# Activation and weight tiles placed at other addresses in the four feed-forward blocks of a decoder trunk

## The chip, the cores and the metric

The kernel runs on one core of a Trainium2 chip. The metric is the device time of one execution in microseconds. The on-chip buffer that the engines read has 128 partitions; an address below is a byte offset within a partition, and it is the same on all 128.

## What is computed

The reference is a decoder trunk of two layers over 256 tokens of width 1024, in float32. Each layer is a feed-forward block, a token mixer with memory attention beside it, and a second feed-forward block. Cut to what matters here:

```python
D_MODEL, SEQ, DEPTH = 1024, 256, 2
D_FF = 256 * ((8 * D_MODEL // 3 + 255) // 256)      # 2816

def swiglu(x, w_in, w_out):
    gate, up = jnp.split(x @ w_in, 2, axis=-1)
    return (jax.nn.silu(gate) * up) @ w_out
...
    for i in range(DEPTH):
        x = x + 0.5 * swiglu(rms_norm(x, ffn1_norm_g[i]), ffn1_w_in[i], ffn1_w_out[i])
        hn = rms_norm(x, mix_norm_g[i])
        ...  # projection, mixer (mLSTM or windowed attention), memory heads, output projection
        x = x + 0.5 * swiglu(rms_norm(x, ffn2_norm_g[i]), ffn2_w_in[i], ffn2_w_out[i])
```

## The kernel before, in words

**Layout.** Activations are kept transposed: 128 features on the partitions, 256 tokens along a row, eight such chunks for the width of 1024. A matmul loads a 128x128 piece of a weight matrix as its stationary operand and streams a 128x256 activation chunk past it; the sum grows in a bank of the accumulation memory. In some groups of the mixers (`rows=True`) the roles are exchanged: a 128x128 piece of the activation is loaded and 256 columns of the weight stream.

**Three products for one.** To keep float32 precision with the faster fp32r matmul, each operand is split into a high part, rounded to fp32r, and a low part, the rest. `mm3` (L224 to L228) issues high by high (L225), high weight by low activation (L226) and low weight by high activation (L227). The activation's parts are made in `Norm.put` (L269 to L280) by `split_gain` (L239), for the input half of a block; the hidden units' parts are made in `hidden` (in `ffn_in`) by `split_plain` (L244) into tiles `u`, for the output half.

**Weights.** `wtile` (L216 to L219) starts a DMA of 128x1024 floats on SyncE's queue into a raw tile `wr` (5 buffers), then `split` (L206 to L214) has ScalarE write the high part into a `wh` tile (L211) and VectorE the low part into a `wl` tile (L212); each of these has 8 buffers, in pools of their own. One weight tile feeds 24 matmuls.

**A feed-forward block** (`ffn`, L509) has two halves. The input half (`ffn_in`, L471) goes through 11 groups of 256 hidden units; each needs four weight tiles (two halves of the width, gate and up). The output half goes through four column blocks of 256 with six weight tiles each (22 hidden chunks); after each, the residual is added and the next block's `Norm.put` is called. `Norm.chain` (L293) runs a little later, among the next block's first matmuls: two matmuls against ones (L296) for the sum of squares, a power on GpSimd, and, after a pause, the broadcast of the inverse root over all partitions by fp32 matmuls (`bcast_rows`, helper `mmf`, L231). An fp32 matmul appears as four passes in the trace.

**Order.** TensorE and SyncE run in the order in which the program issues. A helper class (`Weave`) interleaves side chains, such as `Norm.chain`, by a running clock that each matmul advances. The order is fixed when the program is built. The blocks run as: memory keys and values, block 1, mixer A, block 2, block 3, mixer B, block 4.

**Where tiles lie.** A pool's tiles lie one behind the other, and the pools in the order in which they are made, behind the constants. Before, that order is constants, `xhp` and `xlp` (four tiles of 2,048 bytes each), `up` (31 tiles of 2,048), `vp` (two of 2,080), `wrp` (five of 4,096), `whp` and `wlp` (eight of 4,096 each), `tp`, `sp` (4,864 bytes in all), and small ones. The constants end at byte 28,608.

Of the kernel before, what the change touches and what calls it, by code (L numbers as in the profile page):

```python
# [11 lines left out]
F32R = mybir.dt.float32r  # L12
# [7 lines left out]
P = 128  # L20
T = 256
D = 1024
FF = 2816
# [25 lines left out]
G_MEM, G_F1, G_MIX, G_F2, G_XQ, G_XK, G_AH, G_BQ, G_BK, G_END = 0, 8, 24, 40, 56, 58, 60, 68, 69, 70  # L49
# [6 lines left out]


WARM = 18


class Weave:
# [37 lines left out]
def tile_trunk(ctx: ExitStack, tc: tile.TileContext, a, out):  # L99
# [3 lines left out]
    def mk(pool, shape, dt, tag):  # L103
        seq[0] += 1
        return pool.tile(shape, dt, tag=tag, name=f"{tag}_{seq[0]}")

    def pool(name, bufs, **kw):
        return ctx.enter_context(tc.tile_pool(name=name, bufs=bufs, **kw))

    cst = pool("cst", 1)  # L110
    wv = Weave()


    xhp = pool("xhp", 4)
    xlp = pool("xlp", 4)
    up = pool("up", 31)
    vp = pool("vp", 2)
    wrp = pool("wrp", 5)
    whp = pool("whp", 8)
    wlp = pool("wlp", 8)  # L120
    tp = pool("tp", 7)
    sp = pool("sp", 2)
    ap1 = pool("ap1", 1)
    gp = pool("gp", 1)
    cp = pool("cp", 24)
# [73 lines left out]
    def g(i):  # L199
        return gcol[:, i:i + 1]  # L200
# [2 lines left out]
    pieces = [1]  # L203
    last = [None]

    def split(src, shape):  # L206
        hi = mk(whp, shape, F32R, "wh")
        lo = mk(wlp, shape, F32R, "wl")
        n = shape[1] // pieces[0]
        for i in range(pieces[0]):  # L210
            last[0] = nc.scalar.copy(hi[:, i * n:(i + 1) * n], src[:, i * n:(i + 1) * n])  # L211
            tt(out=lo[:, i * n:(i + 1) * n], in0=src[:, i * n:(i + 1) * n],  # L212
               in1=hi[:, i * n:(i + 1) * n].bitcast(F32), op=ALU.subtract)
        return hi, lo  # L214

    def wtile(src, nk, ncol=256):  # L216
        raw = mk(wrp, [P, nk, ncol], F32, "wr")
        nc.sync.dma_start(raw, src)
        return split(raw, [P, nk, ncol])  # L219

    def wcols(w, c0, kh):
        return wtile(w.rearrange("(k p) f -> p k f", p=P)[:, kh * 4:(kh + 1) * 4, c0:c0 + 256], 4)

    def mm3(ps, wh, wl, xh, xl, start, stop):  # L224
        nc.tensor.matmul(ps, wh, xh, start=start, stop=False, skip_group_check=True)  # L225
        nc.tensor.matmul(ps, wh, xl, start=False, stop=False, skip_group_check=True)  # L226
        nc.tensor.matmul(ps, wl, xh, start=False, stop=stop, skip_group_check=True)  # L227
        wv.now += 0.328  # L228
# [10 lines left out]
    def split_gain(src, gc, hi, lo):  # L239
        act(hi, src, AF.Copy, scale=gc)  # L240
        nc.vector.scalar_tensor_tensor(out=lo, in0=src, scalar=gc, in1=hi.bitcast(F32),
                                       op0=ALU.mult, op1=ALU.subtract)
# [18 lines left out]
    class Norm:  # L261


        def __init__(self, gi, rows=True, half=True):
            self.gi, self.rows, self.half, self.rc = gi, rows, half, None
            self.done = False
            self.xT, self.xh, self.xl = [], [], []

        def put(self, xn):  # L269
            c2 = len(self.xT)  # L270
            hi, lo = mk(xhp, [P, 2, T], F32R, "xh"), mk(xlp, [P, 2, T], F32R, "xl")
            for m in range(2):
                split_gain(xn[:, m], g(self.gi + 2 * c2 + m), hi[:, m], lo[:, m])
            self.xh.append(hi)
            self.xl.append(lo)
            self.xT.append(xn)
            self.square(xn, c2 == 0)
            if c2 == 3:
                self.fold()
# [115 lines left out]

    kT = [mk(cst, [P, 2, T], F32, f"kT{i}") for i in range(2)]
    vM = mk(cst, [P, 2, 512], F32, "vM")
    x0 = Norm(G_F1)

    def memory():  # L400

# [2 lines left out]
        bank = mo()  # L404
        for i in range(WARM):
            nc.tensor.matmul(bank, idle[:, :P], idle, start=True, stop=True, skip_group_check=True)
# [61 lines left out]

    KG = [(0, 4), (4, 4), (8, 4), (12, 4), (16, 4), (20, 2)]

    def ffn_in(x, w_in, hh, hl, mid=None):  # L471

        def hidden(ps):
            t = tmp()
            for m in range(2):
                tt(out=t[:, m], in0=ps[m][:, :T], in1=x.rb, op=ALU.mult)  # L476
            act(t, t, AF.Silu)
            for m in range(2):
                tt(out=t[:, m], in0=t[:, m], in1=ps[m][:, T:], op=ALU.mult)  # L479
            hi, lo = unit(F32R), unit(F32R)  # L480
            split_plain(t, hi, lo)
            hh.append(hi)
            hl.append(lo)

        waiting = []
        for gi in range(11):
            ps = [mo(), mo()]
            for kh in range(2):
                for part in range(2):
                    wh, wl = wcols(w_in, part * FF + gi * 256, kh)  # L490
                    for m in range(2):
                        for k in range(4):
                            kc = kh * 4 + k
                            mm3(ps[m][:, part * T:(part + 1) * T],
                                wh[:, k, m * P:(m + 1) * P], wl[:, k, m * P:(m + 1) * P],
                                x.xh[kc // 2][:, kc % 2], x.xl[kc // 2][:, kc % 2],
                                start=kc == 0 and part == 0, stop=kc == 7)
                        yield
            waiting.append(ps)
            if gi == 0 and not x.done:  # L500
                continue
            yield x.ready
            for ps in waiting:
                hidden(ps)
            waiting.clear()
            if mid is not None and gi == 5:
                wv.spawn(mid())

    def ffn(x, w_in, w_out, nxt=None, mid=None):  # L509

        pieces[0] = 1
        hh, hl = [], []
        yield from ffn_in(x, w_in, hh, hl, mid)
        w = w_out.rearrange("(k p) f -> p k f", p=P)

        def products(ps, m, kg, wt, start):
            ms = slice(m * P, (m + 1) * P)
            for k in range(kg[1]):
                kc = kg[0] + k
                mm3(ps, wt[0][:, k, ms], wt[1][:, k, ms], hh[kc // 2][:, kc % 2], hl[kc // 2][:, kc % 2],  # L520
                    start=kc == 0 and start, stop=kc == 21)

        for c2 in range(4):
            wts = [(kg, w[:, kg[0]:kg[0] + kg[1], c2 * 256:(c2 + 1) * 256]) for kg in KG]
            if nxt is None and c2 == 3:
                wts = [(kg, wtile(src, kg[1])) for kg, src in wts]
                y = tmp()
                for m in range(2):
                    ps = mo()[:, :T]
                    for kg, wt in wts:  # L530
                        products(ps, m, kg, wt, True)
                        yield
                    tt(out=y[:, m], in0=ps, in1=x.hrb, op=ALU.mult)
                    tt(out=y[:, m], in0=y[:, m], in1=x.xT[c2][:, m], op=ALU.add)
                    nc.scalar.dma_start(out[:, 2 * c2 + m], y[:, m])
                return
            ps = mo()
            for kg, src in wts:
                wt = wtile(src, kg[1])
                for m in range(2):  # L540
                    products(ps[:, m * T:(m + 1) * T], m, kg, wt, m == 0)
                    yield
            t = tmp()
            tt(out=t, in0=halves(ps), in1=pair(x.hrb), op=ALU.mult)
            xn = unit(F32)
            tt(out=xn, in0=t, in1=x.xT[c2], op=ALU.add)
            if nxt is None:
                nc.scalar.dma_start(out[:, 2 * c2:2 * c2 + 2], xn)
            else:
                nxt.put(xn)  # L550
        wv.spawn(nxt.chain(), LAT['norm'])


# [95 lines left out]
    def mixer_a(x, nxt):  # L649
        w = a["a_w_in"][0]  # L650
# [26 lines left out]

        raw = mk(wrp, [P, 8, 8], F32, "wr")
        nc.sync.dma_start(raw, w.rearrange("(k p) f -> p k f", p=P)[:, :, 3072:3080])
        gh, gl = mk(whp, [P, 8, P], F32R, "wh"), mk(wlp, [P, 8, P], F32R, "wl")  # L680
        nc.vector.memset(gh.bitcast(F32), 0.0)
        nc.vector.memset(gl.bitcast(F32), 0.0)
        for s in range(2):
# [3 lines left out]
        ps = mo()  # L687
# [60 lines left out]
        for gi in (0, 2, 1, 3):  # L748
            gr = Group(w, gi * 256, x.xh, x.xl)
            yield from gr.all()  # L750
            t = unit(F32)
# [223 lines left out]

    def program():
        yield from memory()
        x1, x2, x3 = Norm(G_MIX, half=False), Norm(G_F2), Norm(G_F1 + 8)
        x4, x5 = Norm(G_MIX + 8, rows=False), Norm(G_F2 + 8)
        yield from ffn(x0, a["ffn1_w_in"][0], a["ffn1_w_out"][0], x1, late_constants)  # L980
        yield from mixer_a(x1, x2)
        yield from ffn(x2, a["ffn2_w_in"][0], a["ffn2_w_out"][0], x3)
        yield from ffn(x3, a["ffn1_w_in"][1], a["ffn1_w_out"][1], x4, rope_tables)
        yield from mixer_b(x4, x5)
        yield from ffn(x5, a["ffn2_w_in"][1], a["ffn2_w_out"][1])

    with tc.manual_schedule(engines={mybir.EngineType.PE, mybir.EngineType.SP}):
        wv.run(program())
# [38 lines left out]
```

## Time and profile before

| | us |
|---|---|
| median of 3 runs | 1012.12 (1012.06 to 1012.26) |
| the profiled execution | 1012.23 |
| its span, first to last instruction | 1010.4 |
| TensorE busy | 998.5 (99%) |
| VectorE busy | 655.5 (65%) |
| ScalarE busy | 519.5 (51%) |
| block 1, matmuls | 33.8 to 215.6 |
| block 2 | 349.6 to 530.2 |
| block 3 | 530.2 to 710.9 |
| block 4 | 825.7 to 1006.3 |

The profile is of one execution. "PE" is TensorE's matmul, "PEld" its weight load; "DVE", "ACT" and "POOL" are VectorE, ScalarE and GpSimd. Matmuls are pipelined, so their durations overlap. In the timeline a line begins with the start in microseconds, then the duration, then engine, line and operands.

### The profile page before, as it was taken

What the parts mean: (1) busy time and instruction counts of PE and PEld (TensorE: products, weight loads), DVE (VectorE), ACT (ScalarE), POOL (GpSimd) and SP (SyncE); (2) the same over time, 40 slices, a digit from 0 to 9 for tenths busy, and PEclk for the clock granted to TensorE, in tenths of its full rate; (3) what the DMA queues carried; (4) which work ended last, traced back from release to release, by engine and by line L of the source; (5) the groups of instructions that cost most, each with busy time, mean ns of one, the idle gap of its engine ahead of it and who ended that gap; (6) DMA issues with size and microseconds to landing.
All of it is one profiled execution on the core that took longest, in us unless ns stands there. A gap on an engine that the chain in (4) does not pass through costs nothing.

```text
span 1010.4 us, 20624 instructions
## 1 busy us (share of the span) xinstructions
PE 998.5 (99%) x8594; PEld 980.2 (97%) x8594; DVE 655.5 (65%) x1063; ACT 519.5 (51%) x764; POOL 35.7 (4%) x32
## 2 busy tenths in 40 slices
PE   8999999999999999999999999999999999999998
PEld 7999999999999999999999999999987899999998
DVE  6866665577856676665558666656787766666551
ACT  7754445446656554444445544544557754454440
POOL 1200000000001000000000000000121000000000
PEclk9999999999999999999999999999999999999999
DMA  9776656666644566665676666567541347666550
GB/s 308 242 245 200 192 180 185 199 183 179 184 139 133 167 210 195 200 189 170 192 206 205 189 191 201 173 197 198 182 131 66 100 131 220 198 189 185 188 170 21
DMA packets 173204, 182.70 MB, mean 181 GB/s; under 512 B 7124, under 2 KB 168328, under 8 KB 173112
## 3 DMA queue, kind: packets, MB, share of 16 engines
q1 hardware_dynamic: 171872, 179.60, 58.3%
q10 hardware_dynamic: 1016, 1.58, 0.5%
q8 instruction: 67, 1.10, 0.5%
q0 software_dynamic: 224, 0.22, 0.2%
q14 instruction: 25, 0.20, 0.1%
HBM read 180.32 MB, written 1.05 MB: 180 GB/s over the span
## 4 chain that ended last, share of the span: by engine, by line
PE 94%; DVE 3%; ACT 1%; DMA 1%; POOL 0%; issue 0%; SPq 0%; ACTq 0%
PE bank L225 30%; PE bank L226 30%; PE bank L227 30%; PE bank L231 2%; PE bank L236 1%; ACT u L132 1%; DVE wl L212 1%; DMA wr<-in_mem_w_kv_dram 1%; PE bank L961 1%; POOL col L379 0%; DVE col L930 0%; DVE u L383 0%; DVE col L591 0%; PE bank L925 0%; DVE u L946 0%
## 5 line engine op out<-in xcount | busy, mean ns | idle before, releaser
L212 DVE TENSOR_TENSOR wl<-wr,wh 128x1024 fp32r<-128x1024 f32 (+1 forms) x347 | 414.7, 1196 | 279.8 <-ACT wh L211 279.0
L211 ACT CAST wh<-wr 128x1024 fp32r<-128x1024 f32 (+1 forms) x347 | 356.8, 1031 | 393.1 <-PE bank L226 368.9
L225 PE MATMUL bank<-xh,wh 128*128 128x256 f32 x1544 | 429.1, 278 | 0.0
L226 PE MATMUL bank<-xl,wh 128*128 128x256 f32 x1544 | 426.8, 276 | 0.0
L227 PE MATMUL bank<-xh,wl 128*128 128x256 f32 x1544 | 426.8, 276 | 0.0
L226 PEld LDWEIGHTS bank<-xl,wh 128*128 128x128 f32 x1544 | 290.3, 188 | 0.1
L225 PEld LDWEIGHTS bank<-xh,wh 128*128 128x128 f32 x1544 | 290.0, 188 | 0.1
L227 PEld LDWEIGHTS bank<-xh,wl 128*128 128x128 f32 x1544 | 289.9, 188 | 0.0
L225 PE MATMUL bank<-u,wh 128*128 128x256 f32 x896 | 249.3, 278 | 0.0
L226 PE MATMUL bank<-u,wh 128*128 128x256 f32 x896 | 247.6, 276 | 0.0
L227 PE MATMUL bank<-u,wl 128*128 128x256 f32 x896 | 247.6, 276 | 0.0
L225 PEld LDWEIGHTS bank<-u,wh 128*128 128x128 f32 x896 | 168.2, 188 | 1.9 <-issue 1.7
L226 PEld LDWEIGHTS bank<-u,wh 128*128 128x128 f32 x896 | 168.4, 188 | 0.1
L227 PEld LDWEIGHTS bank<-u,wl 128*128 128x128 f32 x896 | 168.3, 188 | 0.0
L225 PE MATMUL bank<-wh,xh 128*128 128x256 f32 x208 | 59.7, 287 | 0.0
L226 PE MATMUL bank<-wl,xh 128*128 128x256 f32 x208 | 57.9, 278 | 0.0
L227 PE MATMUL bank<-wh,xl 128*128 128x256 f32 x208 | 57.9, 278 | 0.0
L476 DVE TENSOR_TENSOR t<-bank,rb 128x256 f32<-128x256 f32 x88 | 36.6, 420 | 7.3 <-PE bank L227 7.3
L225 PEld LDWEIGHTS bank<-wh,xh 128*128 128x128 f32 x208 | 39.1, 188 | 0.5 <-issue 0.3
L226 PEld LDWEIGHTS bank<-wl,xh 128*128 128x128 f32 x208 | 39.1, 188 | 0.1
L227 PEld LDWEIGHTS bank<-wh,xl 128*128 128x128 f32 x208 | 39.0, 187 | 0.0
L479 DVE TENSOR_TENSOR t<-t,bank 128x256 f32<-128x256 f32 x88 | 32.7, 412 | 1.8 <-ACT t L132 1.8
(171 smaller groups left out, 657.5 us busy)
## 6 DMA issues: line engine op xcount, KB each, us to landing
wr<-in_ffn_w_in_dram SPq DMA_DIRECT2D x176, 512.0 KB, 3.6
wr<-in_ffn_w_out_dram SPq DMA_DIRECT2D x80, 512.0 KB, 3.5
wr<-in_a_w_in_dram SPq DMA_DIRECT2D x28, 512.0 KB, 3.9
wr<-in_b_w_in_dram SPq DMA_DIRECT2D x14, 512.0 KB, 4.6
wr<-in_a_w_out_dram SPq DMA_DIRECT2D x12, 512.0 KB, 3.3
wr<-in_b_w_out_dram SPq DMA_DIRECT2D x12, 512.0 KB, 3.4
wr<-in_ffn_w_out_dram SPq DMA_DIRECT2D x16, 256.0 KB, 2.8
wr<-in_mem_w_kv_dram SPq DMA_DIRECT2D x7, 512.0 KB, 8.0
```

Of the source, the lines that this page charges most:

```text
L132: ins = nc.scalar.activation(*args, **kw)
L211: last[0] = nc.scalar.copy(hi[:, i * n:(i + 1) * n], src[:, i * n:(i + 1) * n])
L212: tt(out=lo[:, i * n:(i + 1) * n], in0=src[:, i * n:(i + 1) * n], in1=hi[:, i * n:(i + 1) * n].bitcast(F32), op=ALU.subtract)
L225: nc.tensor.matmul(ps, wh, xh, start=start, stop=False, skip_group_check=True)
L226: nc.tensor.matmul(ps, wh, xl, start=False, stop=False, skip_group_check=True)
L227: nc.tensor.matmul(ps, wl, xh, start=False, stop=stop, skip_group_check=True)
L231: nc.tensor.matmul(ps, lhsT, rhs, start=start, stop=stop, skip_group_check=True)
L236: nc.tensor.transpose(ps, src, ident[:k, :k])
L476: tt(out=t[:, m], in0=ps[m][:, :T], in1=x.rb, op=ALU.mult)
L479: tt(out=t[:, m], in0=t[:, m], in1=ps[m][:, T:], op=ALU.mult)
L961: nc.tensor.matmul(o[es[e], cs], vr[:, i, js], pTs[e][:, src], start=i == 0, stop=i == 1, skip_group_check=True)
```

## The change

The activation's high and low parts now lie in one tile `xs` of 16 x 256 + 80 floats, one for each norm, with one buffer: eight high chunks behind one another, then eight low ones, from the offset `at` (in floats) on. The high and low parts of a weight now lie in one tile `w` of 2048 + 128 floats, with eight buffers: the high part from offset `off[0]`, the low part 1024 floats behind it. `off[0]` is set for each half of a feed-forward block and is 0 elsewhere. The pools are made in another order, and `up` has 29 buffers in place of 31. In the diff, `block` only picks the pieces that were picked in place before.

```diff
+XPAD = 80
+WPAD = 128
...
-    xhp = pool("xhp", 4)
-    xlp = pool("xlp", 4)
-    up = pool("up", 31)
     vp = pool("vp", 2)
+
+    up = pool("up", 29)
+    sp = pool("sp", 2)
+    xsp = pool("xsp", 1)
     wrp = pool("wrp", 5)
-    whp = pool("whp", 8)
-    wlp = pool("wlp", 8)
+    wp = pool("wp", 8)
     tp = pool("tp", 7)
-    sp = pool("sp", 2)
...
+    off = [0]
+    def parts(shape):
+        t, n = mk(wp, [P, 2048 + WPAD], F32R, "w"), shape[1] * shape[2]
+        return [t[:, o:o + n].rearrange("p (k f) -> p k f", k=shape[1]) for o in (off[0], off[0] + 1024)]
+
     def split(src, shape):
-        hi = mk(whp, shape, F32R, "wh")
-        lo = mk(wlp, shape, F32R, "wl")
+        hi, lo = parts(shape)
...
-        def __init__(self, gi, rows=True, half=True):
+        def __init__(self, gi, rows=True, half=True, at=64):
...
         def put(self, xn):
             c2 = len(self.xT)
-            hi, lo = mk(xhp, [P, 2, T], F32R, "xh"), mk(xlp, [P, 2, T], F32R, "xl")
+            if c2 == 0:
+                self.tile = mk(xsp, [P, 16 * T + XPAD], F32R, "xs")
+            hi, lo = (self.tile[:, c0:c0 + 2 * T].rearrange("p (m t) -> p m t", m=2)
+                      for c0 in (self.at + 2 * c2 * T, self.at + (8 + 2 * c2) * T))
...
-    x0 = Norm(G_F1)
+    x0 = Norm(G_F1, at=0)
...
-    def ffn(x, w_in, w_out, nxt=None, mid=None):
+    def ffn(x, w_in, w_out, nxt=None, mid=None, offs=(0, 0)):
         pieces[0] = 1
         hh, hl = [], []
+        off[0] = offs[0]
         yield from ffn_in(x, w_in, hh, hl, mid)
+        off[0] = offs[1]
...
+        off[0] = 0
         wv.spawn(nxt.chain(), LAT['norm'])
...
-        x1, x2, x3 = Norm(G_MIX, half=False), Norm(G_F2), Norm(G_F1 + 8)
-        x4, x5 = Norm(G_MIX + 8, rows=False), Norm(G_F2 + 8)
-        yield from ffn(x0, a["ffn1_w_in"][0], a["ffn1_w_out"][0], x1, late_constants)
+        x1, x2, x3 = Norm(G_MIX, half=False), Norm(G_F2, at=0), Norm(G_F1 + 8, at=72)
+        x4, x5 = Norm(G_MIX + 8, rows=False), Norm(G_F2 + 8, at=56)
+        yield from ffn(x0, a["ffn1_w_in"][0], a["ffn1_w_out"][0], x1, late_constants, (16, 16))
         yield from mixer_a(x1, x2)
-        yield from ffn(x2, a["ffn2_w_in"][0], a["ffn2_w_out"][0], x3)
-        yield from ffn(x3, a["ffn1_w_in"][1], a["ffn1_w_out"][1], x4, rope_tables)
+        yield from ffn(x2, a["ffn2_w_in"][0], a["ffn2_w_out"][0], x3, None, (32, 32))
+        yield from ffn(x3, a["ffn1_w_in"][1], a["ffn1_w_out"][1], x4, rope_tables, (0, 48))
         yield from mixer_b(x4, x5)
-        yield from ffn(x5, a["ffn2_w_in"][1], a["ffn2_w_out"][1])
+        yield from ffn(x5, a["ffn2_w_in"][1], a["ffn2_w_out"][1], None, None, (0, 64))
```

More of the change, by code (lines that the diff above doesn't have):

```diff
@@ L222, in wcols, with block @@
         return wtile(w.rearrange("(k p) f -> p k f", p=P)[:, kh * 4:(kh + 1) * 4, c0:c0 + 256], 4)
+    def block(wt, k, m):
+        return [w[:, k, m * P:(m + 1) * P] for w in wt]
     def mm3(ps, wh, wl, xh, xl, start, stop):
@@ L261, in tile_trunk @@
     class Norm:
-        def __init__(self, gi, rows=True, half=True):
-            self.gi, self.rows, self.half, self.rc = gi, rows, half, None
+        def __init__(self, gi, rows=True, half=True, at=64):
+            self.gi, self.rows, self.half, self.rc, self.at = gi, rows, half, None, at
             self.done = False
@@ L469, in tile_trunk, with ffn_in @@
     KG = [(0, 4), (4, 4), (8, 4), (12, 4), (16, 4), (20, 2)]
-    def ffn_in(x, w_in, hh, hl, mid=None):
+    def ffn_in(x, w_in, hh, hl, mid):
         def hidden(ps):
@@ L489, in ffn_in @@
                 for part in range(2):
-                    wh, wl = wcols(w_in, part * FF + gi * 256, kh)
+                    wt = wcols(w_in, part * FF + gi * 256, kh)
                     for m in range(2):
@@ L493, in ffn_in @@
                             kc = kh * 4 + k
-                            mm3(ps[m][:, part * T:(part + 1) * T],
-                                wh[:, k, m * P:(m + 1) * P], wl[:, k, m * P:(m + 1) * P],
+                            mm3(ps[m][:, part * T:(part + 1) * T], *block(wt, k, m),
                                 x.xh[kc // 2][:, kc % 2], x.xl[kc // 2][:, kc % 2],
@@ L507, in ffn_in @@
                 wv.spawn(mid())
-    def ffn(x, w_in, w_out, nxt=None, mid=None):
+    def ffn(x, w_in, w_out, nxt=None, mid=None, offs=(0, 0)):
         pieces[0] = 1
         hh, hl = [], []
+        off[0] = offs[0]
         yield from ffn_in(x, w_in, hh, hl, mid)
+        off[0] = offs[1]
         w = w_out.rearrange("(k p) f -> p k f", p=P)
         def products(ps, m, kg, wt, start):
-            ms = slice(m * P, (m + 1) * P)
             for k in range(kg[1]):
                 kc = kg[0] + k
-                mm3(ps, wt[0][:, k, ms], wt[1][:, k, ms], hh[kc // 2][:, kc % 2], hl[kc // 2][:, kc % 2],
+                mm3(ps, *block(wt, k, m), hh[kc // 2][:, kc % 2], hl[kc // 2][:, kc % 2],
                     start=kc == 0 and start, stop=kc == 21)
@@ L679, in mixer_a @@
         nc.sync.dma_start(raw, w.rearrange("(k p) f -> p k f", p=P)[:, :, 3072:3080])
-        gh, gl = mk(whp, [P, 8, P], F32R, "wh"), mk(wlp, [P, 8, P], F32R, "wl")
+        gh, gl = parts([P, 8, P])
         nc.vector.memset(gh.bitcast(F32), 0.0)
```

## The prediction

> **What bounds the kernel now.** I read the page's shares first, then the chain that ended last, then the waits, and last the timeline of TensorE, because a matmul's duration says little here.
>
> ```profile
> PE 998.5 (99%) x8594; PEld 980.2 (97%) x8594; DVE 655.5 (65%) x1063; ACT 519.5 (51%) x764; POOL 35.7 (4%) x32
> ...
> PEclk9999999999999999999999999999999999999999
> ...
> PE 94%; DVE 3%; ACT 1%; DMA 1%; POOL 0%; issue 0%; SPq 0%; ACTq 0%
> ...
> L225 PE MATMUL bank<-xh,wh 128*128 128x256 f32 x1544 | 429.1, 278 | 0.0
> ...
> L225 PEld LDWEIGHTS bank<-u,wh 128*128 128x128 f32 x896 | 168.2, 188 | 1.9 <-issue 1.7
> ```
>
> TensorE is busy for 99% of the span at full granted clock, and the chain is TensorE for 94%. The three matmuls of the helper mm3 (L225 to L227) are 8112 of its 8594. None of them waits to speak of, and each has a weight load of its own. So the time is the number of matmuls times the distance from one start to the next. The mean durations (278 ns, 188 ns) overlap; the distance must be taken from starts:
>
> ```profile
> 49.76 0.28 PE L225 MATMUL bank<-xh,wh 128*128 128x256 f32 x1
> ...
> 54.35 0.28 PE L225 MATMUL bank<-xh,wh 128*128 128x256 f32 x1
> ```
>
> These starts lie 39 matmuls apart: 4.59 us / 39 = 117.7 ns. Ten microseconds later, with the same tiles:
>
> ```profile
> 59.93 0.28 PE L225 MATMUL bank<-xh,wh 128*128 128x256 f32 x1
> ...
> 64.01 0.28 PE L225 MATMUL bank<-xh,wh 128*128 128x256 f32 x1
> ```
>
> 36 matmuls in 4.08 us: 113.3 ns. There are **two steady distances**, 113.3 (call it the short spacing) and 117.8 ns (the long one), 4.45 ns apart. Each holds without a slip until other work breaks the stream: in block 1 the short one lasts from 55.4 us to the end of the block at 215.6 us. The same two occur where the mixers exchange the roles, so that the weight tile streams and the activation is loaded:
>
> ```profile
> 242.95 0.28 PE L225 MATMUL bank<-wh,xh 128*128 128x256 f32 x1
> ...
> 246.69 0.28 PE L225 MATMUL bank<-wh,xh 128*128 128x256 f32 x1
> ```
>
> ```profile
> 289.91 0.28 PE L225 MATMUL bank<-wh,xh 128*128 128x256 f32 x1
> ...
> 293.80 0.28 PE L225 MATMUL bank<-wh,xh 128*128 128x256 f32 x1
> ```
>
> 33 matmuls each: 3.74/33 = 113.3 and 3.89/33 = 117.9 ns. In the allocation of the kernel before every activation tile starts at 448 past a multiple of 512 bytes (the first xh tile at 28,608 = 55 x 512 + 448) and every weight tile at a multiple of 512. Moving minus loaded address is therefore 448 in normal matmuls, and 64 with the roles exchanged. Both distances occur at both differences, but not equally often. I sorted each entry into a stretch of these matmuls by where it had settled at its tenth one: at 448, 22 stretches short and 15 long; at 64, 1 short and 16 long. After the four broadcast matmuls (L231) that come early in each block, all of 4 stretches (5 with mixer A's) took the short spacing, and kept it for some 888 to 936 more input matmuls and all 528 output matmuls.
>
> **The change, part by part.** The new order of the pools gives, in bytes modulo 512: u at 28,608 + 2 x 2,080 = 32,768, so 0; sp ends at 32,768 + 29 x 2,048 + 4,864 = 97,024, so the xs tile starts at 256; with its 16,704 bytes the raw and split weights start at 64, and 8,704 bytes per w tile is 17 x 512, so each buffer does. With the offsets in the diff (four bytes each), activation minus weight is:
>
> - block 1: input 256 - 128 = 128, output 0 - 128 = 384
> - block 2: input 256 - 192 = 64, output 0 - 192 = 320
> - block 3: input 32 - 64 = 480, output 0 - 256 = 256
> - block 4: input 480 - 64 = 416, output 0 - 320 = 192
>
> Memory and mixers keep 448 (and 64 with exchanged roles). The number, order and operand sizes of all instructions stay. What can change is the distance.
>
> Prices: an input half has 11 x 4 x 2 x 4 x 3 = 1056 matmuls, of which the 936 after the broadcast are one stretch in blocks 2 to 4; an output half has 4 x 2 x 22 x 3 = 528. Put from short to long, an input half costs 936 x 4.45 ns = 4.2 us and an output half 2.3 us. All that has the short spacing in the blocks now, 6336 less 216 in brief long-spaced stretches, would cost 6120 x 4.45 = 27.2 us: the upper end. For the lower end, the shortest distance beside a full weight load is in the fp32 passes:
>
> ```profile
> 54.87 0.44 PE bank L231 x4
> ...
> 364.01 0.44 PE bank L231 x4
> ```
>
> 0.44/4 = 110 ns in the chain. 6336 x 3.3 ns = 21 us less is the other end.
>
> Which value at the new differences? Only 64 has been seen: 16 of 17 entries long, though with exchanged roles. I take block 2's input as long. For 480, which is 32 short of 512, the nearest rows are 448 and 64 on its two sides, with 31 of 54 entries long together; I take long there too, on thin grounds. For 416 the nearest is 448, short after a broadcast: I leave it short. The other five lie far from both rows; a stretch with the short spacing kept it when the difference changed from 448 to 64 without a break (at 241.3 and 710.9 us), and I leave them short. Sum: 2 x 4.2 = **+8.3 us**.
>
> [...]
>
> The rest of the edit I cost at nothing.
>
> ```profile
> ACT wh L211 <- PE bank L226: 368.9, 263, 2.2
> ```
>
> With the high and low part in one tile, the cast of L211 waits for the last reader of the pair, L227 in place of L226: one distance, 0.11 us, later. Behind it in ScalarE's queue are the Silu and the casts of the hidden tiles; ScalarE idled 1.15 to 1.67 us before each of these casts (around 400 us), and 8 weight tiles of 24 matmuls are 8 x 24 x 0.113 = 21.8 us of supply for TensorE. Raw tiles still number 5, 13.6 us of supply against 3.6 us to landing. The u pool falls from 31 to 29 buffers; I counted at most 27 alive, at the first output column (L546). One xs tile replaces four pairs: its first write (L273, under the first output column) comes when the old tile's last reader is at least 132 matmuls (15 us) past, and the matmuls read parts that are written separately. Were the cover gone, TensorE would stand for up to one weight tile's 2.7 us in each block, 11 us in all; nothing suggests a gain.
>
> **Rivals.**
>
> 1. *The address does nothing.* The distance is set by how the stream is entered, and the same broadcast enters it: all halves keep the short spacing, 1012 us. For it: the same two distances to 0.1 ns at 448 and 64, and the short spacing that outlasts a change of difference. Against it: 22 of 37 short at one, 1 of 17 at the other. [...] If the layout did not come out as computed and all halves kept one difference, the result would be here too.
> 2. *The collision goes away far from zero (faster).* Of the sixteen steps of 32 in 512, 448 and 64 are both close to zero. If a moving and a loading stream disturb each other only when their addresses run close, the six halves other than 64 and 480 fall to 110 ns: 2 x 1056 + 4 x 528 = 4224 matmuls x 3.3 ns = 14 us, giving 998; if blocks 2 and 3 pay 8 us as above, 1006. It decides as soon as more than 2500 of the matmuls reach the floor. For it: fp32 passes show that 110 ns can be had with a full weight load. Against it: those passes stream at half the rate (256 columns take 0.86 us for four in the chain at 261.12 us, 215 ns each), and no 256-column fp32r stretch went under 113 ns.
> 3. *The long spacing throughout.* The broadcast's 5 of 5 belongs to 448 alone and an output half keeps what its input half has: three of four blocks long, 3 x 6.5 = 19.5, giving 1032; all, 1039.
>
> **How the numbers follow.** The profiled execution took 1012.23 us, with 1010.4 in its span; the median shown is 1012.12, 0.1 away. 1012.2 + 8.3 = **1020.5 us**. Chances: the forecast and its neighbours, one to five halves long, 0.40; long throughout 0.14; no effect 0.17; faster 0.29. So slower by over 0.2% (2 us, about what a measurement of this kernel can tell from no change) 0.54, within it 0.17, faster 0.29. The range must reach both signs: 998 (rival 2) to 1033 (rival 3 without its last block); the forecast's own is 1014 to 1027.
>
> **What would show it.** In the changed timeline the starts within each half give one distance per half: I expect 117.8 ns in the input halves of blocks 2 and 3, and 113.3 ns in the six others. TensorE's instruction count stays 8594, and no new wait of TensorE on a cast appears. A third distance, near 110 ns or above 118, would make the prediction wrong, as would output halves that go long with their inputs. Stalls of TensorE at the ends of blocks would show that the layout, not the distance, did it.

## The result, and the profile after

The changed kernel takes 1044.24 us (median of 4 executions, 1043.34 to 1045.45) against 1012.19 us before: a ratio of 1.0317, 95% interval 1.0299 to 1.0335. I had forecast 1020.5 us and a range up to 1033 us: the sign was right, the size was not. The profiled execution took 1043.34 us, with a span of 1041.6 us, 31.2 us more than before.

The page of the changed kernel, the lines that answer to those of before:

```profile
PE 1029.2 (99%) x8594; PEld 1011.2 (97%) x8594; DVE 656.0 (63%) x1063; ACT 519.2 (50%) x764; POOL 33.7 (3%) x32
...
PEclk9999999999999999999999999999999999999999
...
L234 PE MATMUL bank<-xs,w 128*128 128x256 f32 x1544 | 434.9, 282 | 0.0
```

The same 8594 matmuls at the same granted clock, and VectorE and ScalarE work as long as before. No new waits in the blocks: TensorE waits for a weight tile only among the memory keys, before 14 us (0.9 us on VectorE in both kernels; on ScalarE 0.3 us before, 0.6 us after), and in the blocks the casts, now waiting for L236 in place of L226 (406.3 us of ScalarE's idle time, against 368.9 before), were never late. Nearly all of the time lies in the distance between matmuls. A table by stage shows it: TensorE's instructions in 50 us of each half. The count in brackets takes in about 2.4 matmuls that began before the window (each lasts 0.28 us, at starts 0.113 to 0.120 apart), so the distance is 50 us / (count - 2.4). Before, the eight halves in order (those left out have 443 or 444 too):

```profile
100.00:150.00 50.00, 50.00 (x443) 1.00 0.62 191
160.00:210.00 50.00, 50.00 (x444) 1.00 0.69 198
...
950.00:1000.00 50.00, 50.00 (x443) 1.00 0.43 132
```

After, all eight (differences 128, 384, 64, 320, 480, 256, 416, 192):

```profile
100.00:150.00 50.00, 50.00 (x423) 1.00 0.57 181
165.00:215.00 50.00, 50.00 (x424) 1.00 0.62 190
400.00:450.00 50.00, 50.00 (x427) 1.00 0.58 184
490.00:540.00 50.00, 50.00 (x427) 1.00 0.60 191
580.00:630.00 50.00, 50.00 (x425) 1.00 0.61 189
678.00:728.00 50.00, 50.00 (x419) 1.00 0.59 184
900.00:950.00 50.00, 50.00 (x424) 1.00 0.59 187
980.00:1030.00 50.00, 50.00 (x426) 1.00 0.39 126
```

443 is 113.5 ns, 427 is 117.8, 424 is 118.6 and 419 is 120.0. No half kept the short spacing. The time from the first start of a half to the first start behind it, less the same of before, is (input, output): block 1 +5.1 and +2.8 us, block 2 +4.2 and +2.3, block 3 +5.0 and +3.5, block 4 +5.4 and +2.3, together 30.7 us; with 0.5 us from outside the blocks that is the whole 31.2 us.

### The profile page after: what moved, and what is told of

Its sections match the earlier page's. It is cut to its first block, busy times and chain, and to the rows that moved or that the text cites. A ratio compares the mean times of both kernels' runs of the same rounds, so it can differ in the third digit from the quotient of the medians.

```text
span 1041.6 us, 20621 instructions
## 1 busy us (share of the span) xinstructions
PE 1029.2 (99%) x8594; PEld 1011.2 (97%) x8594; DVE 656.0 (63%) x1063; ACT 519.2 (50%) x764; POOL 33.7 (3%) x32
## 4 chain that ended last, share of the span: by engine, by line
PE 90%; DVE 5%; ACT 2%; POOL 1%; DMA 1%; issue 1%; SPq 0%; ACTq 0%; POOLq 0%
PE bank L236 29%; PE bank L235 29%; PE bank L234 29%; PE bank L240 2%; DVE w L217 1%; POOL col L392 1%; ACT u L131 1%; DMA wr<-in_mem_w_kv_dram 1%; PE bank L245 1%; DVE col L387 0%; DVE u L960 0%; DVE col L944 0%; DVE u L396 0%; PE bank L975 0%; DVE col L390 0%
## 5 line engine op out<-in xcount | busy, mean ns | idle before, releaser
L217 DVE TENSOR_TENSOR w<-wr,w 128x1024 fp32r<-128x1024 f32 (+1 forms) x347 | 414.8, 1197 | 309.4 <-ACT w L216 308.9
L216 ACT CAST w<-wr 128x1024 fp32r<-128x1024 f32 (+1 forms) x347 | 355.8, 1027 | 426.7 <-PE bank L236 406.3
L234 PE MATMUL bank<-xs,w 128*128 128x256 f32 x1544 | 434.9, 282 | 0.0
L236 PE MATMUL bank<-xs,w 128*128 128x256 f32 x1544 | 433.0, 280 | 0.0
L235 PE MATMUL bank<-xs,w 128*128 128x256 f32 x1544 | 432.7, 280 | 0.0
L235 PEld LDWEIGHTS bank<-xs,w 128*128 128x128 f32 x1544 | 290.8, 188 | 0.1
L236 PEld LDWEIGHTS bank<-xs,w 128*128 128x128 f32 x1544 | 290.6, 188 | 0.0
L234 PEld LDWEIGHTS bank<-xs,w 128*128 128x128 f32 x1544 | 290.5, 188 | 0.1
L234 PE MATMUL bank<-u,w 128*128 128x256 f32 x896 | 253.0, 282 | 0.0
L236 PE MATMUL bank<-u,w 128*128 128x256 f32 x896 | 251.4, 281 | 0.0
L235 PE MATMUL bank<-u,w 128*128 128x256 f32 x896 | 251.2, 280 | 0.0
L234 PEld LDWEIGHTS bank<-u,w 128*128 128x128 f32 x896 | 169.1, 189 | 1.9 <-issue 1.7
L235 PEld LDWEIGHTS bank<-u,w 128*128 128x128 f32 x896 | 169.9, 190 | 0.1
L236 PEld LDWEIGHTS bank<-u,w 128*128 128x128 f32 x896 | 169.1, 189 | 0.0
L234 PE MATMUL bank<-w,xs 128*128 128x256 f32 x208 | 59.8, 288 | 0.0
L236 PE MATMUL bank<-w,xs 128*128 128x256 f32 x208 | 57.9, 279 | 0.0
L235 PE MATMUL bank<-w,xs 128*128 128x256 f32 x208 | 57.9, 279 | 0.0
L234 PEld LDWEIGHTS bank<-w,xs 128*128 128x128 f32 x208 | 39.1, 188 | 0.5 <-issue 0.3
L235 PEld LDWEIGHTS bank<-w,xs 128*128 128x128 f32 x208 | 39.0, 188 | 0.1
L236 PEld LDWEIGHTS bank<-w,xs 128*128 128x128 f32 x208 | 39.0, 188 | 0.0
```

## Experiments

Theory: the difference of the addresses sets which spacings a stream can hold. Rivals: the new layout costs the time; or the difference only decides how a stream settles when it is entered, and what it has taken then lasts. e2, e4 and e6 to e9 are one execution each; distances are read in the profiled execution of each kernel.

**e1: the new layout with 448 everywhere.**

```diff
-    x0 = Norm(G_F1, at=0)
+    x0 = Norm(G_F1, at=64)
...  # at=64 for x2, x3, x5 as well
-        yield from ffn(x0, ..., x1, late_constants, (16, 16))
+        yield from ffn(x0, ..., x1, late_constants, (0, 0))
...  # (0, 0) for the other blocks as well
```

> The changed kernel's pools, shared tiles and buffer counts, but all offsets set so that every activation minus weight is 448 again. If the address difference is what cost the 32 us, all eight halves return to 113.3 ns and the time to 1012 us, within 1 us. If the layout (shared tiles, weights at 64 past a multiple of 512, 29 u buffers) cost it, the time stays near 1044 us. A mixture would lie between, and the excess would be the layout's.

1012.41 us (10 executions), ratio 1.0018 [0.9993, 1.0043]. The layout costs nothing that can be measured; the difference costs the 32 us. Three of the ten executions took 1018.7 to 1020.5 us. The profiled one, of 1018.73, shows why for itself: block 4 came in from the mixer at the long spacing, and had it again after its broadcast, to its end.

```profile
580.00:630.00 50.00, 50.00 (x444) 1.00 0.63 191
880.00:930.00 50.00, 50.00 (x426) 1.00 0.61 185
960.00:1010.00 50.00, 50.00 (x427) 1.00 0.36 114
```

Blocks 3 and 4 of one execution, same code and same difference: entry counts too. Between the two interruptions early in block 4 (the matmuls against ones, and the broadcast), though, this execution had the short spacing:

```profile
834.15 0.50 PE L240 MATMUL bank<-ones,acc 128*128 128x1 f32 x4
834.51 0.36 PE L234 MATMUL bank<-xs,w 128*128 128x256 f32 x1
834.72 0.28 PE L235 MATMUL bank<-xs,w 128*128 128x256 f32 x1
...
839.93 0.28 PE L236 MATMUL bank<-xs,w 128*128 128x256 f32 x1
840.05 0.60 PE L240 MATMUL bank<-con,rc 128*128 128x128 f32 x4
```

46 distances in 5.21 us are 113.3 ns. The kernel before, in the same place, had the long one there and the short one on both sides:

```profile
834.46 0.28 PE L226 MATMUL bank<-xl,wh 128*128 128x256 f32 x1
...
839.87 0.28 PE L227 MATMUL bank<-xh,wl 128*128 128x256 f32 x1
```

46 in 5.41 us are 117.6 ns. So the broadcast does not lead to the short spacing as such. At 448 and 192, with normal roles, each of these interruptions, which come in each block and in mixer A, swapped the two spacings, 113.3 and 117.8 ns, 80 times out of 80 in the traces kept here. Two swaps give a block the spacing that the stream had ahead of the first. At 64 the stream was long, 117.8 ns, after each of 12 such interruptions. Why, no run shows.

The kernel before also took 1018.91 us in one of its executions, and e11 1019.52 us in one; of these there is no trace.

**e2: the seven differences left out.**

```diff
-        x1, x2, x3 = Norm(G_MIX, half=False), Norm(G_F2, at=0), Norm(G_F1 + 8, at=72)
-        x4, x5 = Norm(G_MIX + 8, rows=False), Norm(G_F2 + 8, at=56)
+        x1, x2, x3 = Norm(G_MIX, half=False), Norm(G_F2, at=0), Norm(G_F1 + 8, at=8)
+        x4, x5 = Norm(G_MIX + 8, rows=False), Norm(G_F2 + 8, at=40)
...  # offs of blocks 1 to 4: (48, 104) (24, 72) (0, 40) (0, 0)
```

> The changed kernel with the seven differences it leaves out: block 1 input 0, output 32; block 2 input 96, output 160; block 3 input 224, output 288; block 4 input 352; and 448 in block 4's output. If only the remainder by 128 matters, 0 belongs with 128, 256, 384 (118.7 to 120.0 ns seen there), 32, 160, 288 with 416 (118.8), 96, 224, 352 with 480 (118.4). If each of the sixteen differences has a spacing of its own, some half comes out under 117.7 ns. Block 4's output: if a difference of 448 brings the short spacing by itself (as at 223.7 us of the changed kernel, where 384 went to 448), 113.3; otherwise it inherits about 118. Time: near 1040 us by the first, with 448 in the last half.

1042.8 us (one execution). Over whole halves: 0 gave 120.0 ns, 32 116.7, 96 120.0, 160 117.3, 224 118.3, 288 116.7, 352 120.0; block 4's output at 448 fell to 113.3, out of 120.0. The remainder by 128 does not order them (0 gave 120.0 and 128 gave 118.7). Differences 256 apart do agree, for all but 160 (117.3) and 416 (118.7). 32, 160 and 288 came out under the 117.7 ns that I had named, but far above 113.3.

**e3: 192 everywhere.**

```diff
-    off = [0]
+    off = [64]
...  # at=64 for x0, x2, x3, x5; offs (64, 64) for the four blocks; off[0] = 64 between them
```

> The changed kernel with a difference of 192 everywhere, mixers and memory too (320 with exchanged roles). 192 and 448 leave the same remainder by 128. If the remainder decides what spacings there are and the broadcast's entry decides between them, the halves of the blocks take 113.3 or 117.8 ns as wholes: 1012 us if the broadcast leads to the short one as at 448, about 1038 if to the long one. If 192 allows only 117.8, also about 1038. A third spacing would go against the remainder.

1011.75 us, ratio 0.9995 [0.9986, 1.0005]. All eight halves took 113.3 ns. In the changed kernel 192 ran at 117.8 ns for all of block 4's output; so 192 can do both, and there it took over a stream that was not at the short spacing.

**e4 and e8: entered at 448, then another difference.**

```diff
+            if gi == 3:
+                off[0] = offs[1]
             ps = [mo(), mo()]
...  # x at=64; offs: e4 (0, 96) (0, 32) (0, 64) (0, 80), e8 (0, 80) (0, 48) (0, 72) (0, 120)
```

> The changed kernel, but each block's input half begins at 448, is entered there by the broadcast, and goes over to another difference at its fourth group of 256 hidden units, which also holds for the output half: 64 in block 1, 320 in block 2, 192 in block 3, 128 in block 4. If the difference only decides how an entry settles, and a short spacing lasts once it is there, blocks 1 to 3 keep 113.3 ns to their ends, and the time is 1017 to 1020 us with block 4 at 118.7. If the steady spacing follows from the difference, blocks 1 to 3 go to 117.8 ns right at the fourth group, and the time is near 1035 us.

1020.04 us. Blocks 1 to 3 kept 113.33 ns from the switch to their ends at 64, 320 and 192 (1296 matmuls each). Block 4 came in at the long spacing; at 128 it went to 118.7.

> As in e4_switch each block's input half is entered at 448 and goes over at its fourth group of hidden units, now to differences with another remainder by 128: 128 in block 1, 256 in block 2, 160 in block 3, 480 in block 4, for the output halves too. If these differences cannot hold the short spacing, however the stream was entered, it ends at the fourth group: 118.7 ns at 128, 118.7 or 120.0 at 256, 117.3 at 160, 118.4 at 480, and about 1036 us. If entry alone decides, 113.3 ns goes on in blocks 1 to 3 and the time is 1012 to 1020 us.

1041.23 us. At 128, 256 and 480 the short spacing, held until then, ended at the switch: 118.7, 120.0 and 118.3 ns. Block 3 was entered long in this kernel and took 117.3 at 160, so 160 was not tried from a short one. TensorE of e8 in block 2, from before and after the switch at 391.4 us:

```profile
391.08 0.28 PE L236 MATMUL bank<-xs,w 128*128 128x256 f32 x1
391.19 0.28 PE L234 MATMUL bank<-xs,w 128*128 128x256 f32 x1
391.31 0.28 PE L235 MATMUL bank<-xs,w 128*128 128x256 f32 x1
391.42 0.28 PE L236 MATMUL bank<-xs,w 128*128 128x256 f32 x1
391.53 0.28 PE L234 MATMUL bank<-xs,w 128*128 128x256 f32 x1
391.65 0.28 PE L235 MATMUL bank<-xs,w 128*128 128x256 f32 x1
391.77 0.28 PE L236 MATMUL bank<-xs,w 128*128 128x256 f32 x1
391.89 0.28 PE L234 MATMUL bank<-xs,w 128*128 128x256 f32 x1
```

Starts 0.11 to 0.12 us apart up to 391.53, then 0.12 at each step: no wait, no gap, just another distance, from the first matmul of the new difference (391.53) on. The same stage as counts, e4's block 2 at 320 and e8's at 256:

```profile
400.00:450.00 50.00, 50.00 (x443) 1.00 0.64 194
```

```profile
400.00:450.00 50.00, 50.00 (x419) 1.00 0.57 180
```

Together: some differences (64, 192, 320, 448) can hold either spacing, and kept the short one when a stream brought it; 128, 256 and 480 did not hold it, in one switch each. It is the difference that counts, and neither address alone: 448 held 113.3 ns with the activation at 448 and the weight at 0 (before) and with 0 and 64 (e1), 128 gave 118.7 with 256 and 128 (changed kernel) and with 0 and 384 (e4), and 480 gave 118.3 with 32 and 64 and with 0 and 32 (e8).

**e5: 64 everywhere.**

```diff
-    off = [0]
+    off = [96]
...  # at=64 for x0, x2, x3, x5; offs (96, 96); off[0] = 96 between the blocks
```

> The changed kernel with a difference of 64 everywhere (448 with exchanged roles). 64, 192 and 448 leave one remainder by 128, and the short spacing was held at 64 for 1296 matmuls once it had been entered at 448. If 64 is different only in how an entry settles (block 2's input half took 117.8 ns after the broadcast), all four blocks take 117.8 ns after their broadcasts: about 1039 us. If the remainder by 128 is all that counts and block 2 was an accident of its entry, the blocks behave as at 192: 113.3 ns and 1012 us. Some blocks of each kind, different from one execution to the next, would say that entry is open at 64.

1041.99 us, ratio 1.0290 [1.0272, 1.0307]; every half at 117.8 ns in the profiled execution, and all four executions within 1.4 us. So 64 can hold the short spacing (e4) but did not come out of an interruption with it: after all four broadcasts it had the long one. With exchanged roles (448 here) the stretches from 249.8 and 297.8 us were short, 113.3 ns; at 64 the second had 117.8 in every kernel.

**e6 and e9: steps finer than 32 bytes.**

```diff
...  # e6: x0, x2, x3, x5 at=68, 60, 66, 62; offs (0, 127) (0, 1) (0, 122) (0, 6)
...  # e9: x0, x2, x3, x5 at=58, 59, 54, 52; offs (0, 7) (0, 9) (0, 3) (0, 38)
```

> Steps finer than 32 bytes around 448: block 1 input 464 and output 452, block 2 input 432 and output 444, block 3 input 456 and output 472, block 4 input 440 and output 424; mixers at 448. If the pattern is one of whole 32-byte steps that an address falls into, everything from 448 up to 479 (464, 452, 456, 472) behaves as 448 (113.3 or 117.8 ns), and 424 to 444 as 416 (117 to 119 ns). If the spacing follows the difference smoothly, 444 and 452 stay near 113 and 424 and 472 lie between that and 118. A spacing under 113.3 ns in any half would be a gain of the address that no multiple of 32 gives. Time between 1012 and 1040 us.

1043.42 us. Distances: 464 116.7 ns, 452 118.4 to 119.5 (unsteady), 432 119.3, 444 118.3, 456 120.0, 472 119.2, 440 120.0, and 424 113.35. Four bytes either side of 448 the short spacing was not taken (from streams at 116.7 and 119.3), so 32-byte steps are not the unit, and it is no smooth curve either.

> More steps finer than 32 bytes: block 1 input 424 and output 420, block 2 input 428 and output 412, block 3 input 408 and output 436, block 4 input 400 and output 296 (which is 424 less 128); mixers at 448. In e6_fine 424 held 113.35 ns in an output half, entered from 440 at 120.0 ns. If 424 is a second kind of difference that allows the short spacing, block 1's input takes 113.3 ns after its broadcast, or 117.8 if the entry goes the other way, and 296 shares it if 128 is the period. [...] Time 1020 to 1043 us.

1047.90 us. 424 took 120.0 ns this time, 420 118.3, 428 120.0, 412 120.0, 408 120.5, 436 113.36, 400 116.7, 296 120.0. So 436 can also hold the short spacing, and 424 has two: 113.3 and 120.0. No difference went under 113.3.

**e7: the low parts moved against the high parts.**

```diff
-        return [... for o in (off[0], off[0] + 1024)]
+        return [... for o in (off[0], off[0] + 1024 + low[0])]
...  # the same for xs; (x low, w low) in floats in the input halves: (16, 16) (8, 8) (0, 16) (16, 0)
```

> Which pair of addresses counts: that of a matmul's own operands, or that of the streaming operand and the weight load that runs beside it, for the next matmul? All offsets at 448, but in the input halves the low parts are moved: block 1 both low parts by 64 bytes (beside: 448, 448, 448; own: 448, 0, 384), block 2 both by 32 (beside: all 448; own: 448, 480, 416), block 3 the weight's low part alone by 64 (beside: 448, 384, 448), block 4 the activation's low part alone by 64 (beside: 448, 0, 448). If it is the load beside that counts, input halves 1 and 2 keep 113.3 ns and 3 and 4 lose it (each third matmul at a remainder of 0: 115 to 119 ns). If it is the own pair, all four lose it. Time about 1022 by the first and 1030 by the second.

1038.95 us. No input half had the short spacing: 118.5, 118.9, 118.2 and 117.8 ns. The fourth value is the long spacing, and its stream came from the mixer at 117.8 already, so that half says little. That the matmul and the load beside it (in the kernel before, the load for L226 starts at 59.93 us, with the matmul of L225) stay 448 apart (blocks 1 and 2) is not enough. It speaks for the own pair, or for both pairs, but an address that jumps from one matmul to the next could do the same; which of them it is stays open. The output halves at 448 took 113.3 after blocks 1 and 2 and 117.8 after 3 and 4, which fits that the stream taken over counts.

**e10 to e12: a version that beats both?**

```diff
...  # e10: at=64, off = 6 everywhere (a difference of 424)
...  # e11 from e3, in Group.part (e12 from e1 with 96 and 0 in place of 32 and 64):
+            off[0] = 32 if self.rows else 64
             wt = wt or wcols(self.w, self.c0, kh)
+            off[0] = 64
```

> The changed kernel with 424 everywhere (88 with exchanged roles). If 424 takes a stream to the short spacing from any entry, the blocks run at 113.3 ns throughout, and the time is 1008 to 1011 us, some of the 5 us that the kernel before loses in its long stretches. If it needs a lucky entry as 64 does, whole blocks take 117.8 ns or more and it is 1020 to 1042 us; the exchanged roles at 88 may add up to 3 us, 720 matmuls at 118 instead of 113.

1014.52 us, ratio 1.0017 [1.0007, 1.0027]. In the profiled execution all halves went to 113.3 after the broadcast, but the stretches that were long before ran at 120, as did the exchanged roles at 88.

> As e3_all192, but in the groups with exchanged roles the weights get an offset of their own, so that the streaming minus the loaded address is 192 there too, not 320. In e5_all64, where these groups had 448, the stretches from 249.8 and from 297.8 us ran at 113.3 ns, against 117.8 in the second in every kernel with 64 there. If the sign of the difference is what sends these groups to the long spacing, some 500 to 700 of their matmuls gain 4.4 ns each: 2 to 3 us under e3_all192, 1009 to 1010 us, faster than the kernel before by 0.2%. If what stands before the group decides, it is at 1011.8 us as e3_all192.

1011.69 us, ratio 1.0004 [0.9989, 1.0019].

> As e1_all448, but with 448 in the groups with exchanged roles as well, where it was 64. By the same reasoning 2 to 3 us under e1_all448's shorter executions, 1008.5 to 1010 us. If 448 and 192 differ in nothing but their entries, it agrees with e11_rows192 within 1 us; block 4 may still be entered at the long spacing in some executions, as in e1_all448, which adds 7 us to those.

1012.96 us, ratio 1.0003 [0.9994, 1.0012]. Neither gained. Most of the stretches of exchanged roles that are entered from other work became short, as expected (from 289 us in e11), but two that follow a short stretch without a break became long (from 241 and 710 us), where they had kept it at 320 or 64 (113.3 ns at both places in the kernel before, at 64). No version beat the kernel before by more than the measurement tells.

## Why the prediction was wrong, step by step

- **The bound** was right: time is 8112 matmuls times their distance. The changed addresses moved the span by 31.2 us with TensorE's 8594 matmuls the same.
- **The addresses and the counts** were right; each half had one steady pattern, as I had said it would. Distances above 118, which the prediction named as a sign that it would be wrong, are what came.
- **Block 2's input, long: right**, +4.2 us as priced. e5 shows that the reason held: after a broadcast, 64 was long each time.
- **Block 3's input, long: right in direction**, +5.0 us in place of 4.2, but by luck. The reason was that 480 would do as its neighbours 448 and 64 do; it took 118.3 to 118.4, and did not hold the short one, 113.3, that 448 and 64 held (e8, e4).
- **The step that failed** is "the other five lie far from both rows; a stretch with the short spacing kept it when the difference changed from 448 to 64 without a break (...), and I leave them short", and 416 with them. That row showed something of 64 (e4: also of 320 and 192), and I carried it over to differences that no row showed. It was one-sided even there. "Each holds without a slip until other work breaks the stream" was wrong: where the difference, and with it the roles, went back from 64 to 448, at 252.1 us of the kernel before, the short spacing shown from 242.95 us ended with no other work of TensorE in between:

```profile
252.01 0.28 PE L227 MATMUL bank<-wh,xl 128*128 128x256 f32 x1
252.13 0.28 PE L225 MATMUL bank<-xh,wh 128*128 128x256 f32 x1
...
257.67 0.28 PE L227 MATMUL bank<-xh,wl 128*128 128x256 f32 x1
```

  These are 47 distances in 5.54 us, 117.9 ns; at 33.8 us the same change made a long stretch short (8 distances of 117.5 ns ahead of it, 23 of 113.9 behind it). At 128, 256 and 480 the short spacing ended at the switch (e8: 118.7, 120.0 and 118.3 ns); 320 and 192 kept it in e4 (113.33), but here took over a stream at 117.8 and at 118.7. These six halves, costed at nothing, are 21.5 of the 30.7 us.
- **The ends of the range.** The upper bound of 27.2 us took 117.8 ns as the longest spacing, because no other was in the trace; 118.3 to 120.0 exist, and the excess was 32 us. The range then ended lower still, at 1033 us, because it left out rival 3's last block.
- **Rival 1** (the address does nothing) fell with e1: same layout, 448 restored, 1012.4 us. Its evidence, the short spacing that outlasts a change, was seen at four of the differences (113.3 ns at 64, 192, 320 and 448), and not at every change among them.
- **Rival 2** (no collision far from zero) fell with the result, where 256, the farthest from zero, gave 120.0, and with e2, e6 and e9, where nothing went under 113.3.
- **Rival 3** (long throughout) was nearest. Its conditions came true in part. The short spacing after the broadcast was not 448's alone but 192's too (113.3 ns, e3), 64 did not have it (117.8, e5), and at 448 itself it depended on the stream ahead (e1). No output half of the changed kernel won back the short spacing, though those of blocks 3 and 4 took another distance than their inputs (120.0 ns after 118.4, and 117.8 after 118.7); in e2, 448 did win it back (113.3 after 120.0).
- **The layout's edits at nothing**: right, by e1.

## What to carry over

Where weights are reloaded for every matmul and TensorE sets the time, read the distance between starts stage by stage, not the durations: with the operands at other offsets the same instructions ran 4 to 6% further apart (117.8 to 120.0 ns against 113.3), while the mean duration of the first of the three (L225, L234) went from 278 to 282 ns. Before forecasting a value that no row shows, ask what the row was of; "it held at one other value" is one sample. Here the distance had two values at one difference, 113.3 and 117.8 ns, by what the stream brought and what interrupted it, and ten executions of one kernel took 1011.1 to 1020.5 us (e1): judge a layout in place, over several executions.

## What the runs showed of the hardware

- 256-column fp32r matmuls, each with its own weight load, had steady distances of 113.3, 116.7, 117.3, 117.8, 118.3 to 118.7 and 120.0 ns, by the sixteen multiples of 32 that the difference of streaming and loaded address, modulo 512, can be; most were seen in one or two stretches. None of the sixteen multiples of 32, nor of the fifteen finer values tried, went under 113.3.
- At 64, 192, 320 and 448 two spacings held, 113.3 and 117.8. With the difference and the roles unchanged, a stream kept the one that it had until other work broke it (113.33 ns over the last 888 or 936 input and the 528 output matmuls of each block before). At 448 and 192 the fp32 interruptions early in each block and in mixer A swapped them (80 of 80), and a change from 64 with exchanged roles to 448 moved a stream too (at 33.8 and 252.1 us of the kernel before).
- In the blocks of the kernel before and of the changed one no wait of TensorE shows, yet the distance went from 113.3 up to 120.0 ns with the addresses of the two operands alone: with one layout and the same instructions, 448 everywhere took 1012.41 us (e1) and the changed differences 1044.24. Whether the on-chip buffer or something within TensorE is behind it, no run here shows.
